# Attention probabilities of the neighbourhood layer: 32x32 block transposes on VectorE and 16 SBUF-to-SBUF DMAs per head in place of TensorE transposes and PSUM copies

## The chip, the cores and the metric

The kernel runs on one core of one Trainium2 chip. The metric is the device time of one execution, in microseconds, and the kernel before takes 1547.73 us (the median of three runs).

## The reference, cut to what matters

One step of a trunk of two layers: a layer with neighbourhood attention, then one with grouped-query attention, each followed by a gated feed-forward part. Everything is float32. The change lies in the neighbourhood attention of 512 latent tokens (a grid of 8 rows and 64 columns, 16 heads of 64): each query reads all 8 rows in a window of 16 columns, and 128 context keys, in one softmax.

```python
s_lat = jnp.einsum('brqhd,brkwhd->bhrqkw', qg, kg).astype(jnp.float32) * scale
s_lat = jnp.where(col_ok[None, None, None, :, None, :], s_lat + bias[None], -jnp.inf)
s_ctx = jnp.einsum('brqhd,bchd->bhrqc', qg, k_ctx).astype(jnp.float32) * scale
s = jnp.concatenate([s_lat.reshape(b, h, rows, GRID_W, n_lat), s_ctx], axis=-1)
p = jax.nn.softmax(s, axis=-1).astype(v.dtype)
p_lat = p[..., :n_lat].reshape(b, h, rows, GRID_W, kh, GRID_W)
p_ctx = p[..., n_lat:]
o = jnp.einsum('bhrqkw,brkwhd->brqhd', p_lat, vg) + jnp.einsum('bhrqc,bchd->brqhd', p_ctx, v_ctx)
```

Behind it come the output projection `o @ w_o`, its norm, and the feed-forward part.

## The kernel before, in words

The tokens of the grid are ordered by column, so 128 neighbouring tokens are 16 columns, and there are four such blocks, called slots. A slot's 128 queries lie on the partitions, and its keys are three blocks of 128 out of six (four of the grid, one of the prompt, one, number 5, of the context). So a head has four score tiles of 128 x 384.

`Head.scores(slot)` makes one. Two matmuls (`s<-kh,qs`, `s<-kl,qs`) write it to a PSUM bank, VectorE adds the table of bias and mask and takes the row's minimum (the scores are negated), ScalarE takes the exponential with the row's sum, VectorE takes the reciprocal, and GpSimd scales the row. The result lies in SBUF with the queries on the partitions. The values' matmul needs it the other way, with the keys on the partitions.

`Head.turns(i)` does that. Four TensorE transposes (`tp<-ident,p`) fill a PSUM bank, and one copy (`pk<-tp`, by ScalarE for i = 0 and by VectorE for 1 and 2) brings it to SBUF. A head has three such groups, 12 transposes in all. `values(two)` then multiplies for a pair of heads (`po<-pk,vt`), and ScalarE copies the outcome, in another order of the columns, into `of0[p]`, one of eight tiles that stay in SBUF, where p is the pair. Every fourth head's turn also holds the attention of the prompt's 128 tokens for four heads (steps p0, p1, p2).

TensorE's order is written by hand: the helper `pe` ties every matmul to the one before it, and the lists ORDER0, ORDER and ORDER2 say for a head h what is done in its turn. In them `s0` to `s3` are the scores of head h+1, `t0` to `t2` the transposes of head h, `v` (for an odd h) the values of the pair h-1 and h, `a` a step of the modulation's matrix product (matmuls named `ada`), and `f` a fill: a piece of the projections for later heads (`qk`, `vp`), and when these are used up, of the output projection (`y`, three matmuls of 512 columns a piece). From head 13 on ORDER2 is used. There are 26 pieces left for the heads 13 to 15.

The loads go through SP's queue: the projections' weights (`wsplit`, tiles `wr`, four buffers), the modulation's weights and later ones. A scheduler places them and the other engines' instructions by their priority and their buffers. Each engine and each queue works strictly in its order, so an instruction that waits holds up those behind it. `wsplit` rounds a weight on ScalarE (`wh`) and takes the rest on GpSimd or VectorE (`wl`). `o_split(p)` does the same with `of0[p]` (tiles `oh` and `ol`) before the output projection; it is called after head 11 for p = 0 and 1, after head 12 for 2 to 5, after head 13 for 6, and at the end for 7.

Of the kernel before, what the change touches and what calls it, by code (L numbers as in the profile page):

```python
# [39 lines left out]
NPT = 6  # L40
NPK = 6
# [8 lines left out]
ORDER0 = "f f f t0 s0 f s1 t1 f f t2 f a f f s2 s3 f f f f f".split()  # L50
# [4 lines left out]
ORDER2 = (  # L55
    "t0 s0 s1 f f f t1 f f t2 f s2 f s3 f f f f f f f".split(),
    "p0 s0 s1 f t0 f f t1 f t2 f s2 p1 f s3 v p2 f f f f".split(),
# [47 lines left out]
def hybrid_step(ctx: ExitStack, tc: tile.TileContext, A, O):  # L105
# [367 lines left out]
    of0 = [opool.tile([P, T], F32, name=f"of{p}") for p in range(KC)]  # L473
# [299 lines left out]
    with l_na:  # L773
# [161 lines left out]
        class Head:  # L935


            SRC = {
                0: ((0, 0), (1, 0)), 1: ((1, 1), (2, 0)), 2: ((2, 1), (3, 0)), 3: ((0, 1), (3, 1)),
                4: ((0, 2), (1, 2)), 5: ((2, 2), (3, 2)),  # L940
            }
            BANKS = ((4, 5), (0, 1), (2, 3))
            BLOCK = ((0, 2, 1), (0, 1, 2), (0, 2, 1), (1, 2, 0))
            TABLE = (slice(0, 7, 3), slice(1, 4), slice(1, 6, 2), slice(3, 6))

            def __init__(self, h):
                self.h, self.b = h, h % 2
                self.pts, self.t = [], {}
                self.tb = na_table(h)
                self.nm = sm.tile([P, 4], F32, name="nm")  # L950
                self.su = sm.tile([P, 4], F32, name="su")
                self.rc = sm.tile([P, 4], F32, name="rc")

            def scores(self, slot):
# [7 lines left out]
                pt = ap.tile([P, 384], F32, tag="p", name="p", bufs=NPT)  # L962
                self.pts.append(pt)
# [4 lines left out]
                nc.scalar.activation(pt, sp[:, 0:384], AF.Exp, bias=nm[:, slot : slot + 1],  # L968
                                     scale=-1.0, accum_out=su[:, slot : slot + 1])
# [3 lines left out]
                if not self.h:  # L973
                    plast[:] = [i]

            def turns(self, i):
                tp = bk.get("tp")
                for a, c in enumerate(self.BANKS[i]):
                    for j, (slot, part) in enumerate(self.SRC[c]):
                        n = self.BLOCK[slot][part]  # L980
                        turn(tp[:, (2 * a + j) * P : (2 * a + j + 1) * P],
                             self.pts[slot][:, n * P : n * P + P], ident)
                x = self.t[i] = ap.tile([P, 512], F32, tag="pk", name="pk", bufs=NPK)
                if i:
                    nc.vector.tensor_copy(x, tp)
                else:
                    nc.scalar.copy(x, tp)
                bk.put(tp)

        def values(two):  # L990
# [3 lines left out]

            def block(ov, c, x):
                for v in two:
                    rows_ = slice(64 * v.b, 64 * v.b + 64)
                    mm(ov[rows_], vt[:, c, v.h % 4, :], x(v), start=c == 5, stop=c == 3)

            block(po, 5, lambda v: v.t[0])  # L1000
            for i in (1, 2):
                for a, c in enumerate(Head.BANKS[i]):
                    ov = po[:, c * P : c * P + 256] if c < 3 else po.rearrange("p (a b) -> p a b", b=P)[:, 0::3, :]
                    block(ov, c, lambda v: v.t[i][:, a * 256 : a * 256 + 256])
            om = of0[two[0].h // 2][:, 0:NS].rearrange("p (r c) -> p r c", c=GW)
# [59 lines left out]
        for slot in range(4):  # L1065
            head.scores(slot)
            fill(slot < 3)
        for h in range(H):
# [4 lines left out]
            for i, step in enumerate(order):  # L1073
# [7 lines left out]
                elif step[0] == "t":  # L1081
                    head.turns(int(step[1]))
# [879 lines left out]
```

## Time and profile before

| what | value |
|---|---|
| time, median of 3 runs (lowest to highest) | 1547.73 us (1546.61 to 1548.59) |
| span of the profiled execution, first to last instruction | 1546.0 us |
| median of the runs less that span | 1.7 us |
| TensorE busy in the span | 1512.8 us, 98% |
| attention stage, first exponential to the last pair's values | from 69.9 to 321.4 us |
| granted TensorE clock, mean | 0.999 |

An execution's span runs from its first to its last instruction; the profile gives no other time of that execution. A group's row has the line, the engine, the operation, the tile that is written and those that are read, the shapes and the count, then its busy time and the mean of one, and the idle time of the engine before them with what ended it. A row of the timeline has the start, the duration and the count of merged instructions. Matmuls overlap, so the pace of TensorE is read from start to start. In a fp32 matmul the profile shows two passes, so the 10 matmuls of a pair's values are 20 there.

### The profile page before, as it was taken

How to read it: one execution, taken by the hardware profiler on the slowest of the kernel's cores; microseconds unless marked ns; L12 is line 12 of the kernel's file. 1: busy time of each engine (PE TensorE's matmuls, PEld its weight loads, DVE VectorE, ACT ScalarE, POOL GpSimd, SP SyncE). 2: the span in 40 equal slices, each digit the busy share in tenths (PEclk: the TensorE clock that was granted, in tenths of full speed). 3: DMA queues.
4: the chain of work that ended last, by engine and by line, in shares of the span. 5: the costliest groups of instructions: out<-in, count | busy, mean ns of one | idle time of the engine just before them, and what ended most of it. 6: DMA issues, size and time to landing. Idle time of an engine off the chain costs nothing.

```text
span 1546.0 us, 26097 instructions
## 1 busy us (share of the span) xinstructions
PE 1512.8 (98%) x9709; PEld 1344.4 (87%) x9709; DVE 1024.1 (66%) x1648; ACT 854.2 (55%) x1624; POOL 701.8 (45%) x606
## 2 busy tenths in 40 slices
PE   6999999999999999999999999999999999999998
PEld 5988998888999999978887878878899999988886
DVE  4553453659877666756757877773988887786554
ACT  5665564646655555654544447763666655554443
POOL 1554463432355455525444464532235666542433
PEclk9999999999999999999999999999999999999999
DMA  9745454253565665388574421015433334447664
GB/s 318 210 122 159 122 132 116 64 190 124 183 224 177 221 190 162 114 277 272 178 234 155 129 69 42 2 40 190 153 114 115 119 111 156 132 164 252 226 221 131
DMA packets 196666, 243.99 MB, mean 158 GB/s; under 512 B 11484, under 2 KB 153020, under 8 KB 196540
## 3 DMA queue, kind: packets, MB, share of 16 engines
q1 hardware_dynamic: 186704, 235.74, 47.7%
q10 hardware_dynamic: 9836, 6.59, 2.5%
q8 instruction: 76, 1.25, 0.3%
q14 instruction: 50, 0.41, 0.1%
HBM read 214.38 MB, written 26.34 MB: 156 GB/s over the span
## 4 chain that ended last, share of the span: by engine, by line
PE 66%; DVE 5%; ACT 2%; issue 2%; POOL 1%; DMA 1%; POOLq 0%; DVEq 0%; ACTq 0%
PE acc L117 19%; PE ux L117 18%; PE uz L117 8%; PE gp L117 5%; PE uy L117 4%; PE po L117 3%; PE y L117 3%; PE s L117 2%; PE tp L120 2%; PE ada L117 1%; DMA wr<-in_ffn_w_up 1%; DVE t L1281 1%; ACT gp L1692 1%; PE tr L120 0%; DVE xo L400 0%
## 5 line engine op out<-in xcount | busy, mean ns | idle before, releaser
L180 POOL TENSOR_TENSOR wl<-wr,wh 128x1024 fp32r<-128x1024 f32 x70 | 173.3, 2480 | 238.5 <-ACT wh L178 223.5
L1204 POOL TENSOR_TENSOR wl<-wr,wh 128x1024 fp32r<-128x1024 f32 x76 | 183.5, 2435 | 46.9 <-ACT wh L1203 43.3
L117 PE MATMUL ux<-B,wh 128*128 128x322 f32 x832 | 200.1, 311 | 0.9 <-ACT u L1258 0.9
L1281 DVE SCALAR_TENSOR_TENSOR t<-C,cw,t 128x644 f32<-128x644 f32 x176 | 156.3, 888 | 51.3 <-ACT t L1279 50.7
L117 PE MATMUL acc<-wh,alo 128*128 128x512 f32 x440 | 172.3, 392 | 0.3 <-DVE alo L1173 0.3
L178 ACT CAST wh<-wr 128x1024 fp32r<-128x1024 f32 x140 | 145.6, 1048 | 48.5 <-DMA wr<-in_ffn_w_down 37.4
L117 PE MATMUL acc<-wh,ahi 128*128 128x512 f32 x440 | 171.9, 391 | 0.0
L117 PE MATMUL acc<-wl,ahi 128*128 128x512 f32 x440 | 171.8, 391 | 0.0
L117 PE MATMUL uz<-B,wh 128*128 128x322 f32 x640 | 156.2, 312 | 0.9 <-ACT v L1258 0.9
L117 PEld LDWEIGHTS ux<-B,wh 128*128 128x128 f32 x832 | 143.6, 189 | 3.4 <-issue 1.2
L1173 DVE TENSOR_TENSOR alo<-ain,ahi 128x384 fp32r<-128x384 f32 (+1 forms) x88 | 84.0, 973 | 84.9 <-ACT ahi L1171 84.0
L117 PE MATMUL ux<-B,wl 128*128 128x322 f32 x416 | 129.5, 311 | 2.7 <-DVE wl L1204 2.7
L117 PE MATMUL qk<-hT,wh 128*128 128x384 f32 (+1 forms) x512 | 122.4, 315 | 0.0
L117 PEld LDWEIGHTS uz<-B,wh 128*128 128x128 f32 x640 | 110.9, 189 | 4.3 <-ACT v L1258 1.5
L1204 POOL TENSOR_TENSOR vl<-wr,vh 128x1024 fp32r<-128x1024 f32 x38 | 96.3, 2535 | 24.6 <-ACT vh L1203 24.3
L1203 ACT CAST wh<-wr 128x1024 fp32r<-128x1024 f32 x84 | 84.8, 1049 | 40.8 <-DVE wr L1227 40.5
L1279 ACT ACTIVATE t<-C,cw 128x644 f32<-128x644 f32 x88 | 78.6, 893 | 47.8 <-DVE C L1309 40.3
L180 DVE TENSOR_TENSOR wl<-wr,wh 128x1024 fp32r<-128x1024 f32 x70 | 91.3, 1315 | 20.1 <-ACT wh L178 19.5
L117 PE MATMUL uz<-B,wl 128*128 128x322 f32 x320 | 99.6, 311 | 0.3 <-POOL wl L1204 0.3
L117 PEld LDWEIGHTS acc<-wh,alo 128*128 128x128 f32 x440 | 82.5, 188 | 18.8 <-DVE alo L1173 1.1
L117 PEld LDWEIGHTS acc<-wl,ahi 128*128 128x128 f32 x440 | 82.6, 188 | 17.9
L117 PEld LDWEIGHTS acc<-wh,ahi 128*128 128x128 f32 x440 | 82.6, 188 | 17.8
(259 smaller groups left out, 3857.7 us busy)
## 6 DMA issues: line engine op xcount, KB each, us to landing
wr<-in_ffn_w_up SPq DMA_DIRECT2D x88, 512.0 KB
wr<-in_ffn_w_down SPq DMA_DIRECT2D x88, 512.0 KB
wr<-in_ada_w SPq DMA_DIRECT2D x72, 512.0 KB
act<-act SPq DMA_DIRECT2D x44, 321.0 KB
wr<-in_na_w_qkv SPq DMA_DIRECT2D x24, 512.0 KB
mod<-modrow SPq DMA_DIRECT2D x20, 512.0 KB
ain<-act SPq DMA_DIRECT2D x44, 192.0 KB
wf<-in_ada_w SPq DMA_DIRECT2D x16, 512.0 KB
```

The lines of the kernel that those rows point to most:

```text
L117: pe(nc.tensor.matmul(*a, **k))
L120: pe(nc.tensor.transpose(*a, **k))
L178: i = nc.scalar.copy(hi, raw)
L180: j = (low or nc.vector).tensor_sub(lo, raw, f32(hi))
L1173: pin(nc.vector.tensor_sub(lo[:, 0 : c1 - c0], ain[:, 0 : c1 - c0], f32(hi[:, 0 : c1 - c0])))
L1203: nc.scalar.copy(hl[0], src)
L1204: low.tensor_sub(hl[1], src, f32(hl[0]))
L1279: nc.scalar.activation(t, taps(0), AF.Identity, bias=cw[:, 3, n : n + 1], scale=cw[:, 1, n : n + 1])
L1281: nc.vector.scalar_tensor_tensor(t, taps(d), cw[:, w, n : n + 1], t, op0=ALU.mult, op1=ALU.add)
L1692: nc.scalar.activation(self.pt[i].rearrange("p (a b) -> p a b", a=2), sv, AF.Exp, bias=nm, scale=-1.0, accum_out=su)
```

## The change

The probabilities of a head lie in one tile `p4` of 128 x (4 x 4 x 3 x 32): for a slot, four groups k of 3 x 32 columns, so that the 32 columns of group k of each of the three key blocks stand together. The exponential writes in that order. After GpSimd's scaling VectorE transposes the tile in 32x32 blocks, in place (`nc.vector.transpose(pt, pt)`, once a slot). A block's keys then lie on the partitions of the query block q where it stood, and `exchange()` moves each of the 16 pieces of 32 partitions x 384 elements from (partitions q, group k) of `p4` to (partitions k, group q) of a second tile `px`. It is called once a head, behind the scores of slot 3, and issues its 16 DMAs on SP's queue. `values` reads `px` through an access pattern of 2 x 4 x 32 elements (`block`); the context's product, one matmul of 512 columns, becomes two of 256.

```diff
             def scores(self, slot):
...
-                nc.scalar.activation(pt, sp[:, 0:384], AF.Exp, bias=nm[:, slot : slot + 1],
-                                     scale=-1.0, accum_out=su[:, slot : slot + 1])
+                nc.scalar.activation(pt.rearrange("p k n i -> p n k i"),
+                                     sp[:, 0:384].rearrange("p (n k i) -> p n k i", n=3, k=4), AF.Exp,
+                                     bias=nm[:, slot : slot + 1], scale=-1.0, accum_out=su[:, slot : slot + 1])
...
-            def turns(self, i):
-                tp = bk.get("tp")
...
+                nc.vector.transpose(pt, pt)
+
+            def exchange(self):
+
+                self.px = ap.tile([P, 4, 4, 3, QD], F32, tag="px", name="px", bufs=NPX)
+                for q in range(4):
+                    for k in range(4):
+                        nc.sync.dma_start(self.px[QD * k : QD * k + QD, q], self.p4[QD * q : QD * q + QD, k])
+
+            def block(self, s0, s1):
+
+                c0 = 3 * QD * s0[0] + QD * s0[1]
+                c1 = 3 * QD * s1[0] + QD * s1[1]
+                return raw_ap(self.px, c0, [self.px.ap[0], [c1 - c0, 2], [12 * QD, 4], [1, QD]])
```

`p4` and `px` have two buffers each. To make room, `of0` has four buffers in place of eight tiles. The first four pairs' tiles go to DRAM after their pair, and `o_split` reads them back:

```diff
+    def of_store(p):
+
+        of0d[p] = dr.tile([P, T], F32, name=f"of0d{p}")
+        nc.sync.dma_start(of0d[p], of0.pop(p))
...
         def o_split(p):
             hi, lo = osp0[p]
-            nc.scalar.copy(hi, of0[p])
-            nc.vector.tensor_sub(lo, of0[p], f32(hi))
+            if p in of0d:
+                x = wp.tile([P, T], F32, tag="wr", name="ofr")
+                nc.sync.dma_start(x, of0d[p])
+            else:
+                x = of0[p]
+            nc.scalar.copy(hi, x)
+            nc.vector.tensor_sub(lo, x, f32(hi))
```

The lists lose the steps t0 to t2, gain `x` for the next head's exchange, and spread the scores; the number of fills in a head stays. The two of ORDER for even and odd heads:

```diff
-    "f f t0 s0 f s1 t1 f f t2 f a f f s2 s3 f f f f f f".split(),
-    "p0 f f t0 s0 f s1 t1 f t2 p1 f f f v a p2 s2 s3 f f f".split(),
+    "f s0 f f s1 f f s2 f f a f s3 f f f x f f f".split(),
+    "p0 f s0 f f s1 f p1 f f s2 f f v a p2 s3 f f x".split(),
```

Two places show what becomes of the order. The first is TensorE at the end of the stage, the last 24 projection matmuls and the values of heads 14 and 15. Before:

```order
L117 MATMUL y_3781<-wl,oh_3620 128x512
L117 MATMUL y_3781<-wh,ol_3621 128x512
L120 MATMUL tp<-ident,p 128x128 x4
L117 MATMUL y_3820<-wh,oh_3620 128x512
L117 MATMUL y_3820<-wl,oh_3620 128x512
L117 MATMUL y_3820<-wh,ol_3621 128x512
L120 MATMUL tp<-ident,p 128x128 x8
L117 MATMUL po<-pk,vt 64x512 x2
L117 MATMUL po<-pk,vt 64x256 x6
L117 MATMUL po<-pk,vt 64x2x128 x2
```

Now the same engine, from the last piece of projection to the first one behind the values:

```order
L119 MATMUL y_3804<-wh,oh_3621 128x512
L119 MATMUL y_3804<-wl,oh_3621 128x512
L119 MATMUL y_3804<-wh,ol_3622 128x512
L119 MATMUL po<-px,vt 64x256 x10
L119 MATMUL po<-px,vt 64x2x128 x2
```

The three groups of transposes of head 15 are gone, and the values stand directly behind the projection: between the scores of slot 3 of head 15 and the values are 24 matmuls `y`, where there were 27 and 12 transposes.

The second is SP's queue from the output projection's weights to the first load of the next stage (`mod`). Before:

```order
L293 DMA wr<-in_ada_w 128x1024 x2
L174 DMA wr<-in_na_w_o 128x2x512 x2
L293 DMA wr<-in_ada_w 128x1024 x2
L174 DMA wr<-in_na_w_o 128x2x512
L293 DMA wr<-in_ada_w 128x1024 x2
L174 DMA wr<-in_na_w_o 128x2x512 x4
L352 DMA mod<-modrow_2_83 128x1024
```

And now, where `px<-p` are the exchanges of the heads 12, 13, 14 and 15 and `ofr<-of0d` the tiles that come back from DRAM:

```order
L176 DMA wr<-in_na_w_o 128x2x512 x2
L994 DMA px<-p 32x384 x16
L1027 DMA ofr<-of0d_2200 128x640
L1027 DMA ofr<-of0d_2597 128x640
L994 DMA px<-p 32x384 x16
L176 DMA wr<-in_na_w_o 128x2x512 x5
L994 DMA px<-p 32x384 x32
L354 DMA mod<-modrow_2_83 128x1024
```

The exchanges now stand among the loads of one queue, those of the heads 14 and 15 behind each other and ahead of the next stage's first load. The same holds further up, where each head has its 16 between the projections' weights.

More of the change, by code (lines that the diff above doesn't have):

```diff
@@ L39 @@
 QW = T + 64
-NPT = 6
-NPK = 6
+NPT = 2
+NPX = 2
+NOF = 4
+QD = 32
 NAR = 2
@@ L1067, in hybrid_step @@
             fill(slot < 3)
+        head.exchange()
         for h in range(H):
```

63 lines of the change are left out of this document (27 added, 36 removed).

## The prediction

> **What bounds the kernel now.** I read the page first (engine shares, chain), then the table of stretches over the attention stage, then the waits of PE and of the SP queue inside that stage.
>
> ```profile
> span 1546.0 us, 26097 instructions
> PE 1512.8 (98%) x9709; PEld 1344.4 (87%) x9709; DVE 1024.1 (66%) x1648; ACT 854.2 (55%) x1624; POOL 701.8 (45%) x606
> PE 66%; DVE 5%; ACT 2%; issue 2%; POOL 1%; DMA 1%; POOLq 0%; DVEq 0%; ACTq 0%
> ```
>
> TensorE is busy for 98% of the span and carries most of the chain that ends last. The stretches of the stage (columns: length, then busy time of PE, PEld, DVE, ACT, POOL with the number of instructions, clock, DMA share, GB/s) say the same of the place that is edited:
>
> ```profile
> 100.00:150.00 50.00, 50.00 (x405) 43.97 (x403) 19.75 (x60) 27.27 (x74) 24.10 (x25) 1.00 0.52 142
> 250.00:300.00 50.00, 48.39 (x346) 41.99 (x340) 26.65 (x72) 29.91 (x78) 21.62 (x25) 1.00 0.33 91
> 300.00:330.00 30.00, 30.00 (x160) 23.87 (x159) 12.21 (x22) 14.18 (x34) 6.93 (x13) 1.00 0.18 60
> PE tp L120 <- DVE qs L878: 1.4, 2, 1.0
> SPq L174 <- POOL wl L180: 159.9, 21, 20.9
> ```
>
> PE has no idle time there to speak of (its longest wait is 1.0 us), DVE is busy for about half, and SP's queue stands still for 159.9 us, waiting for buffers of weights. So a PE instruction taken out here shortens the run by what it occupies, as long as nothing makes PE wait in its place.
>
> **What is removed.** 16 heads x 12 transposes, and three PSUM copies per head.
>
> ```profile
> L120 PE MATMUL tp<-ident,p 128*128 128x128 f32 x192 | 29.2, 273 | 2.0 <-DVE qs L878 1.4 <-POOL p L972 0.7
> 262.18 0.60 PE L120 MATMUL tp<-ident,p 128*128 128x128 f32 x4
> 262.53 0.37 PE L117 MATMUL qk<-hT,wh 128*128 128x256 f32 x1
> 262.74 0.28 PE L117 MATMUL qk<-hT,wl 128*128 128x256 f32 x1
> 262.85 0.40 PE L117 MATMUL qk<-hT,wh 128*128 128x256 f32 x2
> L985 DVE COPY pk<-tp 128x512 f32<-128x512 f32 x32 | 21.6, 685 | 9.2 <-PE tp L120 8.9
> ```
>
> The mean of 273 ns overlaps the next one, so I go by starts. Four transposes take 262.18 to 262.53 = 0.35 us, and the qk behind them takes 0.21 us to the next start, where the one after it takes 0.11: another 0.10 us lost at the change of kind. There are 48 such groups: 48 x 0.35 = 16.8 us at least, 48 x 0.45 = 21.6 at most. Three groups stand beside another group and lose less: I take **-20 us**. The DVE copies (21.6 us) and ACT's 16 stand beside PE's work and are worth nothing in themselves.
>
> **The values' matmuls.** They read px in runs of 32 elements where they read pk in one piece; the columns stay the same, 6 x 256 for 512 + 4 x 256 a head. The nearest rows of PE (qk, s) run at one pace whatever their pieces; I take 0, with -1 and +3 as ends.
>
> **What is added on DVE.** 64 block transposes of 128x384. No row shows one; the 128x512 copy above (685 ns) and the 162 ns reciprocal bound it, and 3/4 of the copy gives 0.5 us, which I take. 64 x 0.5 = 32 us of DVE against 21.6 taken away, on an engine that is half idle. But each transpose waits for POOL's scaling with DVE's next instructions (qs, kl, the next score's bias) behind it; I allow **+1.5 us** in all for PE meeting a late one, ends 0 and 8.
>
> The Trainium skill, "VectorE: DVE Perf Modes", section "Rules for kernel authors", says to transpose 128x128 on TensorE when PSUM is an acceptable destination, so it speaks against this change. Its table gives 311 ns on VectorE for a 128x128 bf16 block grid against 390 ns on TensorE; here TensorE's start-to-start is 0.35 / 4 = 88 ns. By the page's figure a 128x384 one would be an estimated 0.93 us with both ends 0.4 us later and the sum about 1 us worse; no run here shows it.
>
> **What is added on SP: the exchange.** 16 DMAs per head. The code waits for the transpose of the head's last slot, issues 16 in a row, and the values of a pair need the second head's last one to have landed. The length of that path against PE's work meanwhile decides the case. First the softmax of one slot in the trace:
>
> ```profile
> 94.95 0.34 PE L117 MATMUL s<-kl,qs 128*128 128x384 f32 x1
> 95.53 0.57 DVE L964 CUSTOM_DVE_ANT_0 s<-s,tb 128x384 f32<-128x384 f32 x1
> 96.55 0.57 ACT L968 ACTIVATE p<-s,nm 128x384 f32<-128x384 f32 x1
> 98.68 0.17 DVE L971 RECIPROCAL rc<-su 128x1 f32<-128x1 f32 x1
> 99.10 0.59 POOL L972 TENSOR_SCALAR p<-p,rc 128x384 f32<-128x384 f32 x1
> ```
>
> From the score's end (95.3) to POOL's end (99.7) are 4.4 us; without the queues in between the durations alone make 2.2. With the transpose I take 4.7 us, ends 3 and 6.5. Then the issue of 16 DMAs, by the nearest rows of SP's queue (duration min/median/max in ns, first and last start), and how long after an issue the last one lands:
>
> ```profile
> L1169 SPq DMA_DIRECT2D ain<-act x88: 319/347/1398, 639.0 to 1521.2; - x88
> L1564 SPq DMA_DIRECT2D gkh<-gkh x12: 590/590/1025, 846.5 to 866.0; - x12
> 82.66 0.82 SPq L293 DMA_DIRECT2D wr<-in_ada_w  x2
> 863.94 0.59 SPq L1564 DMA_DIRECT2D gkl<-gkl  x1
> 864.62 0.59 SPq L1564 DMA_DIRECT2D gkh<-gkh  x1
> SPq L1958 <- DMA out_y_prompt<-xo: 1.6, 1, 1.6
> ```
>
> px is 32 partitions of one run of 384 elements. ain is the nearest in shape (rows of up to 384 elements, 0.35 us; two plain loads in a row take 0.82, so **0.40 us** from one to the next). gkh is the nearest in kind (SBUF to SBUF), but has three dimensions on both sides: 0.68 us from one to the next. I take 0.40 and keep 0.68. Landing: 1.6 us for 256 KB. The path is 4.7 + 15 x 0.40 + 0.35 + 1.6 = **12.7 us**.
>
> Now PE's work meanwhile. Period of a pair of heads, and what it holds:
>
> ```profile
> 99.81 2.81 PE L117 MATMUL po<-pk,vt 128*64 128x512 f32 x20 [0.24 <-DVE qs L878]
> 102.54 1.07 PE L117 MATMUL ada<-wr,scolp 128*32 128x256 f32 x16
> 104.41 0.34 PE L117 MATMUL s<-kl,qs 128*128 128x384 f32 x1
> 104.59 0.34 PE L117 MATMUL s<-kh,qs 128*128 128x384 f32 x1
> 266.33 2.81 PE L117 MATMUL po<-pk,vt 128*64 128x512 f32 x20
> ```
>
> Five periods are 266.33 - 99.81, one is 33.3 us. Less six groups of transposes (2.7), the values (2.8), eight slots at 2 x 0.18 (2.9) and two ada steps (2.1) leaves 22.8 us for 24 fills: 0.95 each. In the changed orders 14 fills and 3 slots stand between an odd head's slot 3 and the values: 14 x 0.95 + 1.1 = **14.4 us**. That hides 12.7, by 1.7 us, for the six pairs up to head 11: **0**.
>
> The pair 12/13 has less: 36 y matmuls, 8 prompt scores, 3 slots and a prompt transpose. The tail has the least: 24 y, since the fills run out.
>
> ```profile
> 313.13 0.39 PE L117 MATMUL y<-wh,oh 128*128 128x512 f32 x1
> 316.31 0.39 PE L117 MATMUL y<-wh,ol 128*128 128x512 f32 x1
> 317.68 1.03 PE L120 MATMUL tp<-ident,p 128*128 128x128 f32 x8
> 318.64 2.81 PE L117 MATMUL po<-pk,vt 128*64 128x512 f32 x20
> ```
>
> From 313.13 to 316.31 are 14 steps of y: 0.23 us each. Pair 12/13: 36 x 0.23 + 8 x 0.11 + 1.1 + 0.4 = 10.7, so PE waits 12.7 - 10.7 = **+2.0 us**. Pair 14/15: 24 x 0.23 = 5.5, so it waits 12.7 - 5.5 = **+7.2 us**; before, eight transposes stood there and nothing waited. All of SP's later loads (mod, the up-projection's first weights) stand behind these exchanges, but a wait of PE moves the time they are needed as well: 0.
>
> A long pause may also cost speed. At the run's start PE comes out of one:
>
> ```profile
> 17.77 3.64 PE L120 MATMUL tr<-ident,x 128*128 128x128 f32 x16 [1.54 <-DVE x L541]
> 21.34 2.24 PE L117 MATMUL row<-wf,scolp 128*32 128x256 f32 x32
> 33.52 1.93 PE L117 MATMUL row<-wf,scolp 128*32 128x256 f32 x32
> ```
>
> Sixteen transposes take 3.64 us, 0.23 each against 0.12 in the 317.68 row; after those 3.6 us the pace is nearly the later one (2.24 against 1.93). So some 1.8 us go after a long pause: **+1.5 us** for the tail's, ends 0 and 3. The granted clock in the stretches is 1.00 all along and shows none of it. The Trainium skill, "TensorE: Matmul & The Clock Gate", section "Why this matters for your kernels", says that idle gaps above some 3 us drop the array to half its clock; the slow transposes agree with it, and without that rule the sum would be 1.5 us lower.
>
> The four of-tiles that go to DRAM and come back are 8 DMAs on SP. The reloads for heads 4 to 7 stand behind px of head 12 on SP, ahead of their splits on ACT and DVE: I reckon them at 0, because the fills that need them come after the prompt scores, with an end of +3.
>
> **Sum.** -20 + 1.5 + 2.0 + 7.2 + 1.5 = **-7.8 us**. Against the profiled execution's span of 1546.0: 1538.2. The shown runs' median is 1547.73, 1.7 us above that span, so the forecast is **1540 us**.
>
> **Rivals.**
> 1. *SP's issue becomes the bound* (slower). If each exchange DMA costs what gkh costs, the path is 4.7 + 15 x 0.68 + 0.59 + 1.6 = 17.1 us. Six pairs wait 17.1 - 14.4 = 2.7 (16), pair 12/13 waits 6.4, and the tail 11.6 plus about 3 because px of head 14 is still being issued; with eight pauses of 1 us of slow clock that is +45 - 20 = +25: 1573 us. For it: the only SBUF-to-SBUF rows. Against: kinds with a plain 2-D shape all cost 0.32 to 0.35. From the forecast, the wins are used up at an issue of about 0.55 us: the two ends take 30 us per us of issue, and the six pairs 90 more from 0.51 us on.
> 2. *Half-way: the gain is given back.* The softmax path is 6.5 us, since DVE waits for a POOL that is in a weight split, and the issue costs 0.43. The path is then 15.0 us: six pairs wait 0.6 each (3.5), both ends 2.3 more (4.5): -7.8 + 8 is no change, 1548, with 1545 to 1552 around it. For it: the row of 99.10, where POOL came late. Against: the 1.7 us in hand.
> 3. *All is hidden.* The path is 10 us (softmax 3, landing 0.8, issue 0.39): the tail waits 4.5, nothing else does, the clock stays: 1546.0 - 21 + 4.5 + 1.7 = 1531.
> That the change doesn't do what it says is excluded by the order of PE, which has no tp of p left.
>
> **How the numbers follow.** Forecast (1536 to 1544) 0.48, rival 1 0.25, rival 2 0.20, rival 3 0.07. About 0.2%, 3 us, is what a measurement here can tell from no change. Faster takes the forecast less 0.04 at its edge, rival 3 and 0.02 of rival 2: 0.53. Same takes 0.04 and 0.11: 0.15. Slower takes the rest of rival 2 and rival 1: 0.32. The two sides both weigh, so: the forecast's own range is 1536 to 1544, and the one that leaves 2 in 10 out is **1532 to 1565** (it takes in the lower part of rival 1).
>
> **What would show it.** Right: no tp of p, PE idle before po only, nearly all of it in the last pair (7 us) and the one before (2 us), px issues 0.40 us apart, the six earlier pairs without a wait. Wrong: px issues 0.6 us apart and PE waiting for a DMA at every po (rival 1); DVE idle for POOL's scaling and PE waiting for qs or kl (rival 2); a transpose near 0.9 us.

## The result, and the profile after

The changed kernel takes 1592.6 us (median of five runs, 1590.9 to 1596.6), against 1547.9 us for the kernel before beside it: 1.0292 times the time, 95% interval 1.0280 to 1.0305. The forecast was 1540 us with a range from 1532 to 1565. It is 45 us slower, and beyond the rival that had the sign right (1573 us).

The page of the changed kernel, its span, its engines and its chain:

```profile
span 1590.1 us, 26190 instructions
PE 1510.3 (95%) x9549; PEld 1338.5 (84%) x9549; DVE 1036.0 (65%) x1680; ACT 845.3 (53%) x1608; POOL 700.0 (44%) x606
PE 62%; DVE 6%; ACT 2%; issue 2%; POOL 1%; DMA 1%; POOLq 0%; DVEq 0%; ACTq 0%; SPq 0%
```

TensorE's busy time fell by 2.5 us only although 192 transposes are gone: matmuls at a lower clock count as busy for longer. (In a run below without exchange and turns, where the clock of the stage is 1.00, it is 1492.3 us, 20.5 less than before.) The waits of TensorE from 60 to 372 us (sum, times, longest) and two stretches (columns as in the prediction) say what it lost:

```profile
PE po L119 <- DMA px<-p: 32.4, 8, 9.6
PE s L119 <- DVE qs L892: 5.6, 1, 5.6
PE tp L122 <- POOL pp L708: 4.0, 2, 2.2
...
100.00:150.00 50.00, 39.77 (x309) 35.24 (x309) 18.53 (x53) 21.15 (x56) 22.70 (x23) 0.94 0.61 161
...
350.00:376.00 26.00, 16.40 (x76) 12.26 (x76) 5.92 (x5) 8.63 (x18) 6.69 (x7) 0.80 0.52 160
```

Before, no wait here was above 1.0 us and the clock was 1.00. Now there are 32.4 us of waits for `px`, some 16 us of other ones, and a granted clock of 0.94 and, at the end, 0.80. The values of four pairs on the timeline; the last score and the last turn of the second pair's odd head; and SP's queue around that pair and at the end:

```profile
107.93 2.78 PE L119 MATMUL po<-px,vt 128*64 128x256 f32 x22 [0.96 <-DMA px<-p]
147.57 4.57 PE L119 MATMUL po<-px,vt 128*64 128x256 f32 x22 [8.14 <-DMA px<-p]
329.43 3.10 PE L119 MATMUL po<-px,vt 128*64 128x256 f32 x23
360.10 4.13 PE L119 MATMUL po<-px,vt 128*64 128x256 f32 x22 [9.60 <-DMA px<-p]
...
125.08 0.34 PE L119 MATMUL s<-kl,qs 128*128 128x384 f32 x1
129.45 0.58 DVE L987 STREAM_TRANSPOSE p<-p 128x384 f32<-128x384 f32 x1 [0.72 <-POOL p L984]
...
115.82 14.69 SPq L994 DMA_DIRECT2D px<-p  x16
130.61 1.37 SPq L295 DMA_DIRECT2D wr<-in_ada_w  x2
132.08 13.67 SPq L994 DMA_DIRECT2D px<-p  x16
...
338.25 20.21 SPq L994 DMA_DIRECT2D px<-p  x32
```

At the second pair, the even head's exchange holds SP from 115.82 to 130.51, the odd head's starts only behind it and ends at 145.75, and TensorE goes on at 147.57, 1.8 us later. At five of the eight pairs the same 22 matmuls take 4.1 to 4.6 us behind their wait in place of 2.78: the pause costs a second time, through the clock. Around the second pair the granted clock is 0.50 in each stretch of 1 us from 147 to 151 us, 0.89 in the next and then 1.00. The whole of `px` on SP's queue (ns min/median/max) and two of SP's waits from 60 to 376 us:

```profile
L994 SPq DMA_DIRECT2D px<-p x256: 507/588/1545, 78.9 to 357.9; - x128
SPq L994 <- DMA wr<-in_ada_w: 10.7, 8, 3.4
SPq L176 <- POOL wl L182: 10.4, 3, 8.2
```

An issue takes 0.59 us, and 16 in a row 10.0 us at best, 0.63 apart; where they also wait for earlier loads it is up to 14.7. SP had 159.9 us to spare in front of buffers of weights and now has 10.4. That row (SP's line of the weights waiting for `wl`) is used below as the measure of SP's slack.

The other new wait, in the order of time:

```profile
78.17 2.52 POOL L941 TENSOR_TENSOR tb<-mask,tr 128x256 f32<-128x256 f32 x3
80.65 2.36 POOL L182 TENSOR_TENSOR wl<-wr,wh 128x1024 fp32r<-128x1024 f32 x1
82.99 0.58 POOL L984 TENSOR_SCALAR p<-p,rc 128x384 f32<-128x384 f32 x1
83.61 0.58 DVE L987 STREAM_TRANSPOSE p<-p 128x384 f32<-128x384 f32 x1 [3.49 <-POOL p L984]
87.39 0.66 PE L119 MATMUL s<-kh,qs 128*128 128x384 f32 x1 [5.63 <-DVE qs L892]
```

GpSimd is in the tables of the next heads and a weight split, so the scaling comes late, the turn behind it makes VectorE wait 3.49 us, and `qs`, which stands behind the turn, makes TensorE wait 5.63 us. A turn itself takes 0.58 us.

### The profile page after: what moved, and what is told of

Its sections match the earlier page's. It is cut to its first block, busy times and chain, and to the rows that moved or that the text cites. A ratio compares the mean times of both kernels' runs of the same rounds, so it can differ in the third digit from the quotient of the medians.

```text
span 1590.1 us, 26190 instructions
## 1 busy us (share of the span) xinstructions
PE 1510.3 (95%) x9549; PEld 1338.5 (84%) x9549; DVE 1036.0 (65%) x1680; ACT 845.3 (53%) x1608; POOL 700.0 (44%) x606
## 4 chain that ended last, share of the span: by engine, by line
PE 62%; DVE 6%; ACT 2%; issue 2%; POOL 1%; DMA 1%; POOLq 0%; DVEq 0%; ACTq 0%; SPq 0%
PE acc L119 18%; PE ux L119 16%; PE uz L119 8%; PE gp L119 5%; PE uy L119 4%; PE po L119 2%; PE y L119 2%; PE s L119 2%; PE tp L122 2%; PE ada L119 1%; DMA wr<-in_ffn_w_up 1%; DVE t L1298 1%; ACT gp L1709 1%; DVE al L1221 0%; ACT t L1296 0%
## 5 line engine op out<-in xcount | busy, mean ns | idle before, releaser
L119 PEld LDWEIGHTS acc<-wh,ahi 128*128 128x128 f32 x440 | 82.6, 188 | 17.7
```

What stands on the lines that cost most here:

```text
L119: pe(nc.tensor.matmul(*a, **k))
```

## The experiments

All are edits of the changed kernel; the line numbers in their rows are their own. Ratios are to the kernel before, run beside them. Those that leave out the exchange or the turns, or move its pieces straight across or by halves, do not compute the full result.

### Without the exchange

```diff
-NPT = 2
+NPT = 4
...
-                self.px = ap.tile([P, 4, 4, 3, QD], F32, tag="px", name="px", bufs=NPX)
-                for q in range(4):
-                    for k in range(4):
-                        nc.sync.dma_start(self.px[QD * k : QD * k + QD, q], self.p4[QD * q : QD * q + QD, k])
+                self.px = self.p4
```

> Leaves out the exchange: the values' matmuls read each head's turned blocks where they are (no DMA, four buffers of p in place of two of p and two of px). The turns on VectorE and all waits for GpSimd's scaling stay. Theory A (the 16 DMAs per head on SP's queue, 0.59 us each, hold PE at the values): all of the 32 us of PE waits for px go, and with them the half-speed stretches behind them; left is the gain of the transposes taken out, less what the turns cost: 1526 to 1535 us. Theory B (VectorE's turns waiting in order for GpSimd hold up the score chain, and with it everything): 1570 us or more, since that part stays. Theory C (the values' matmuls themselves are slower, by reading px in runs of 32): po rows stay at 4 us in place of 2.8, 1555 us or more.

1548.4 us, 0.9998 (0.9988 to 1.0007). The exchange costs 1592.6 - 1548.4 = 44 us. But without it the kernel is not faster than before, against the 1526 to 1535 us of theory A; its waits of TensorE:

```profile
PE tp L122 <- POOL pp L708: 5.0, 4, 2.6
PE s L119 <- DVE qs L892: 4.9, 1, 4.9
...
L119 PE MATMUL po<-p,vt 128*64 128x256 f32 x192 | 22.5, 383 | 1.9 <-DVE qs L892 1.9
```

So the gain of 20 us is lost to something else, and theory C is out: a `po` matmul takes 383 ns, as long as the 256-column ones before (379).

### The same bytes, 4 DMAs a head

```diff
                 for q in range(4):
-                    for k in range(4):
-                        nc.sync.dma_start(self.px[QD * k : QD * k + QD, q], self.p4[QD * q : QD * q + QD, k])
+                    nc.sync.dma_start(self.px[:, q], self.p4[:, q])
```

> The same bytes (768 KB a head) go from p to px, but by 4 DMAs of 128 partitions x 384 elements in place of 16 of 32 x 384; the pieces are copied straight across, not exchanged. Theory A, in the form that a DMA from SBUF to SBUF costs SP some 0.6 us whatever its size: an exchange takes 2.5 us of SP in place of 10 to 14, only the tail pair waits (3 to 5 us): 1530 to 1540 us. Theory D (the bytes: moving 768 KB from SBUF to SBUF beside the weights' loads is what takes the time): stays at 1585 to 1595 us.

1549.7 us, 1.0009 (1.0000 to 1.0018): within 1.3 us of no exchange at all, and with the changed kernel's two buffers of p, so the four buffers of the run above were not what helped. The bytes cost nothing that can be told; the 43 us above it come with the step from 4 to 16 DMAs.

```profile
L993 SPq DMA_DIRECT2D px<-p x64: 464/593/1678, 78.3 to 315.1; - x64
```

A DMA of four times the size takes SP the same 0.59 us. (The forecast of 1530 to 1540 had the lost 20 us in it too.)

### 16 DMAs of another shape

```diff
-                        nc.sync.dma_start(self.px[QD * k : QD * k + QD, q], self.p4[QD * q : QD * q + QD, k])
+                        nc.sync.dma_start(self.px[:, q, k], self.p4[:, q, k])
```

> Again the same bytes, by 16 DMAs a head as in the change, but each of 128 partitions x 96 elements, straight across. Theory A by count (a price per DMA): px issues stay 0.6 us apart and the time stays within 5 us of the changed kernel, 1588 to 1600 us. If instead the price comes from the narrow shape (32 partitions, so few rows for the engines to share), an issue falls to 0.35 to 0.4 us and the time to about 1540 to 1560 us.

1575.8 us, 1.0175 (1.0158 to 1.0192), between the two forecasts.

```profile
L994 SPq DMA_DIRECT2D px<-p x256: 464/599/1523, 75.2 to 343.3; - x128
```

The price of an issue is the same, so the narrow shape is not the cause. The 17 us less go with an earlier start: a DMA here reads one slot alone, and the first ones of a head leave before its last slot is done (SP's waits for the turn are 15.2 us in place of 37.3). This run changes two things against the changed kernel, so that these 17 us are due to the start is not shown. Against the run with four DMAs, which copies straight across too, the 16 DMAs cost 26 us in spite of the earlier start.

### 8 DMAs a head

```diff
-                    for k in range(4):
-                        nc.sync.dma_start(self.px[QD * k : QD * k + QD, q], self.p4[QD * q : QD * q + QD, k])
+                    for k in range(2):
+                        nc.sync.dma_start(self.px[64 * k : 64 * k + 64, q], self.p4[64 * (1 - k) : 128 - 64 * k, q])
```

> The same bytes by 8 DMAs a head of 64 partitions x 384 elements (the two halves swapped, not the exchange of 32-blocks). Theory A2 (SP's time, some 0.65 us per DMA): an exchange takes 5 to 6 us of SP, two of them 11 of 33 us, which leaves room: close to the run with four DMAs, with 3 to 6 us at the last pair: 1550 to 1558 us. If the loss grows in step with the number of DMAs (1550 us at 4, 1593 at 16): about 1564 us.

1558.7 us, 1.0068 (1.0055 to 1.0081), just above the 1550 to 1558 us of A2 and below the 1564 of a price in step with the count. The same bytes thus take 1549.7, 1558.7 and 1592.6 us in 4, 8 and 16 DMAs: four more than 4 cost 9 us, and eight more than 8 another 34. SP's slack (its wait for `wl`) is 62.1, 32.3 and 10.4 us in the three.

### Without the turns

```diff
-                nc.vector.transpose(pt, pt)
```

> Leaves out the 64 block transposes on VectorE; the 16 DMAs a head stay and wait for GpSimd's scaling instead. Theory A: the exchange starts 0.6 to 1 us earlier at each of the eight pairs, and the one score that waited 5.6 us for qs behind a turn comes in time: 8 to 15 us less than the changed kernel, 1577 to 1585 us; the 16 issues stay as long. Theory B: most of the loss goes, 1560 us or less.

1582.1 us, 1.0227 (1.0204 to 1.0249), 10 us below the changed kernel, inside theory A. TensorE's waits for `px` stay at 30.6 us.

### Neither exchange nor turns

```diff
-                nc.vector.transpose(pt, pt)
...
+                self.px = self.p4
```

> Leaves out both the exchange and the turns on VectorE: the values read the scaled p where it is, and nothing of the change is left but the 192 transposes taken off TensorE. If the prediction's term of -20 us is right, and the run without the exchange (1548 us) gave it all back through VectorE's turns that wait in order for GpSimd: 1524 to 1532 us, with no PE wait over 2 us in the stage. If the transposes on TensorE were worth less than reckoned (5 us or so, since PE cannot run through the rest faster than its inputs come): 1540 us or more.

1538.7 us, 0.9937 (0.9919 to 0.9955), between the two. The turns cost 1548.4 - 1538.7 = 10 us, and the transposes gave 9 us, not 20. What is left of waits in the stage:

```profile
PE tp L122 <- POOL pp L708: 5.7, 2, 3.1
PE tk L122 <- ACT kp L906: 1.7, 1, 1.7
PE qk L119 <- DVE qs L892: 1.2, 1, 1.2
```

These are 8.6 us, where the kernel before has 3.0 us of waits. The clock is below 1.00 in four of the stretches from 60 to 376 us (0.95, 0.98, 0.97 and 0.93), an estimated 6 us at most. Together that is 11 to 12 us for the 11 that are missing. `pp` is the softmax of the prompt's four heads. Before, three groups of transposes stood between its scores (p0) and its turn (p1), besides the same four fills and two slots.

### The prompt's turn later

```diff
-    "p0 f s0 f f s1 f p1 f f s2 f f v a p2 s3 f f x".split(),
+    "p0 f s0 f f s1 f f f p1 s2 f f v a p2 s3 f f x".split(),
```

(the same in ORDER2, on the kernel with neither exchange nor turns)

> Leaves out exchange and turns, as the run at 1539 us did, and moves the prompt's four transposes two fills later in the order of the odd heads. There PE waited 5.7 us for GpSimd's pp, which 12 transposes a head had covered in the kernel before. If that lost cover is why only 9 of the 20 us came through: that wait falls below 1.5 us and the time to 1531 to 1535 us. If PE loses the time elsewhere as soon as it runs faster: 1537 us or more.

1536.1 us, 0.9923 (0.9906 to 0.9939); the wait for `pp` falls to 1.9 us and the clock of the stage is 1.00 throughout. A part of the lost cover, 2.6 us, comes back. The run misses its forecast by 1 us: 7.9 us of waits are left, spread over the stage, 1.9 of them for `pp`.

### The scaling on VectorE

```diff
-                i = nc.gpsimd.tensor_scalar(pt, pt, rc[:, slot : slot + 1], 1.0, op0=ALU.mult, op1=ALU.mult)
-                if not self.h:
-                    plast[:] = [i]
+                nc.vector.tensor_scalar(pt, pt, rc[:, slot : slot + 1], 1.0, op0=ALU.mult, op1=ALU.mult)
```

(without the exchange; what `plast` orders is tied to a table of head 1 instead)

> Without the exchange, as in the first run, but the scaling of p by 1/sum moves from GpSimd to VectorE, directly ahead of the turn, so that no VectorE instruction waits for GpSimd's queue; VectorE gets 64 instructions of some 0.56 us more. Theory B1 (the 20 us went into the in-order wait for GpSimd): the PE waits for qs, kl and pp fall from 16 to below 5 us: 1528 to 1536 us. Theory B2 (it is VectorE's added load itself): with 36 us more on VectorE it gets no better than 1548, rather 1550 us or more.

1543.9 us, 0.9972 (0.9960 to 0.9983): 4.5 us of the 10 come back although VectorE has more to do, which neither forecast has. A `s` still waits 3.3 us for `qs`; the row of all the scalings and a place on the timeline show why:

```profile
L986 DVE TENSOR_SCALAR p<-p,rc x64: 380/421/2510, 72.6 to 310.4; 128x384 f32<-128x384 f32 x64
...
78.47 2.40 POOL L182 TENSOR_TENSOR wl<-wr,wh 128x1024 fp32r<-128x1024 f32 x1 [1.07 <-ACT wh L180]
78.57 2.51 DVE L986 TENSOR_SCALAR p<-p,rc 128x384 f32<-128x384 f32 x1
```

A scaling of 0.42 us takes 2.51 us when it starts 0.1 us behind GpSimd's weight split, and ends 0.2 us after it. It is no single case: the 18 scalings that start while a weight split runs all end 0.21 to 0.23 us behind it. With the scaling moved, VectorE no longer waits for GpSimd's result, but here still for GpSimd.

### Each turn one slot later

```diff
+                while late:
+                    late.pop(0)()
                 nc.vector.reciprocal(rc[:, slot : slot + 1], su[:, slot : slot + 1])
...
-                nc.vector.transpose(pt, pt)
+                late.append(lambda: nc.vector.transpose(pt, pt))
```

(without the exchange; the last one is issued where the exchange stood)

> Without the exchange, as in the first run; GpSimd keeps the scaling, but the turn of a slot is issued on VectorE only after the next slot's bias and maximum (where VectorE waits for ScalarE's exp in any case), not right behind its own scaling. The same work on every engine. Theory B1 (the 10 us between the runs with and without turns, 1548 and 1539 us, are VectorE waiting in order for GpSimd): back to 1539 to 1543 us. If it is the 37 us of turns themselves: 1546 us or more.

1549.3 us, 1.0006 (0.9996 to 1.0015). It says nothing on either theory, since the edit did not do what it was for: VectorE's idle time ahead of the turns for the scaling is 56.1 us, against 55.7 without the edit. At the place shown above the turn is still ahead of `qs` and waits 3.52 us. The scheduler orders VectorE's instructions, and it left this turn where it was.

### One turn a head, where the exchange stood

```diff
-                nc.vector.transpose(pt, pt)
...
+                nc.vector.transpose(self.p4, self.p4)
+                self.px = self.p4
```

> Without the exchange, as in the first run (1548 us), in the order of the changed kernel; the four turns of each head become one VectorE instruction of 128x1536 where the exchange stood, two or three fills behind the last score. Theory B1 (a VectorE queue that stands behind a late GpSimd scaling is what the turns cost): most of the 10 us between 1548 and 1539 come back, 1539 to 1544 us. If the turns cost by their length: VectorE has 16 x 1.78 = 28 us in place of 37, so at most 2 us come back, 1546 us or more.

1548.7 us, 1.0008 (0.9999 to 1.0017): nothing comes back. That is outside theory B1 and inside the forecast by length (1546 us or more).

```profile
L990 DVE STREAM_TRANSPOSE p<-p 128x1536 f32<-128x1536 f32 x16 | 28.5, 1779 | 17.7 <-POOL p L984 17.7
...
89.45 1.67 POOL L941 TENSOR_TENSOR tb<-mask,tr 128x256 f32<-128x256 f32 x2 [4.47 <-DMA tr<-in_k_rpb]
91.09 0.59 POOL L984 TENSOR_SCALAR p<-p,rc 128x384 f32<-128x384 f32 x1
91.71 1.78 DVE L990 STREAM_TRANSPOSE p<-p 128x1536 f32<-128x1536 f32 x1 [4.21 <-POOL p L984]
93.98 0.33 PE L119 MATMUL sp<-kl,qs 128*128 128x128 f32 x1 [4.04 <-DVE kl L864]
```

VectorE's waits for the scaling fell from 55.7 to 17.7 us in sum, and the time did not follow. What counts are the few long ones: here GpSimd waits 4.47 us for a table's load, the scaling and the turn stand behind it, and `kl` behind the turn, so that one TensorE wait of 4.9 us was only exchanged for one of 4.0. This shows why the late turn did not help; it does not exclude that the length of the turns counts as well.

### Through DRAM, 5 DMAs

```diff
+                d = dr.tile([P, 16 * 3 * QD], F32, name=f"pd{self.h}")
+                nc.sync.dma_start(d, self.p4.rearrange("p a b c d -> p (a b c d)"))
+                w = 12 * QD
+                for k in range(4):
+                    nc.sync.dma_start(
+                        self.px[QD * k : QD * k + QD].rearrange("p q s n j -> p q (s n j)"),
+                        raw_ap(d, w * k, [[4 * w, QD], [4 * w * QD, 4], [1, w]]),
+                    )
```

> The exchange made through DRAM: one write of 768 KB and four reads of 192 KB a head, 5 DMAs on SP in place of 16. Five issues of 0.4 to 0.6 us are 2 to 3 us, and the two landings (read after write) an estimated 2 x 2 to 4 us, worked out from 256 KB loads that land in 1.6 us: a path of 6 to 11 us behind the last turn. Theory A (the number of DMAs on SP): the six inner pairs do not wait, the last pair 3 to 6 us: 1548 to 1558 us, since the 20 us given back by the turns remain. Rival (a DMA behind a DMA costs as much as ten issues): px waits stay above 20 us, 1575 us or more.

1609.4 us, 1.0407 (1.0384 to 1.0429). Theory A's forecast is wrong here, and the rival holds: TensorE waits 39.2 us for `px`. The issues are cheap:

```profile
L996 SPq DMA_DIRECT2D px<-pd x64: 302/424/1455, 82.8 to 373.9; - x64
L993 SPq DMA_DIRECT2D pd<-p x16: 326/327/345, 78.2 to 369.3; - x16
...
122.94 0.33 SPq L993 DMA_DIRECT2D pd<-p  x1
129.88 1.74 SPq L996 DMA_DIRECT2D px<-pd  x4
```

But the reads must wait for the write, and SP waits with them, 6.9 us here, with the loads behind it standing still. A few long DMAs on the path cost as much as many short ones.

### Every second DMA from ScalarE's queue

```diff
-                        nc.sync.dma_start(self.px[QD * k : QD * k + QD, q], self.p4[QD * q : QD * q + QD, k])
+                        (nc.scalar if k % 2 else nc.sync).dma_start(
+                            self.px[QD * k : QD * k + QD, q], self.p4[QD * q : QD * q + QD, k])
```

> The 16 DMAs of a head as in the change, every second one issued from ScalarE's queue. Theory A (the issue on one queue, one after the other): the issue falls from 10 us to about 5 a head and px waits to below 10 us; but ScalarE, in order, then waits for the turn and spends 8 x 0.6 = 4.8 us a head on issuing, with qs, kh and exp behind it: 1560 to 1580 us. Rival (a limit that both queues share): px waits stay at 30 us, 1590 us or more.

1616.3 us, 1.0442 (1.0420 to 1.0464). The waits for `px` fall from 32.4 to 6.4 us, as theory A said, but its time of 1560 to 1580 us was wrong: the kernel is slower than with one queue.

```profile
PE tk L122 <- ACT kp L906: 20.8, 4, 7.9
...
ACT kp L906 <- DMA px<-p: 35.0, 3, 13.5
ACT vt L501 <- DMA px<-p: 30.2, 3, 10.7
```

ScalarE's copies stand behind its share of the exchange for up to 13.5 us at a time.

### The values later

```diff
-    "f s0 f f s1 f f s2 f f a f s3 f f f x f f f".split(),
-    "p0 f s0 f f s1 f p1 f f s2 f f v a p2 s3 f f x".split(),
+    "f s0 f f s1 f v X f s2 f f a f s3 f f f x f f f".split(),
+    "p0 f s0 f f s1 f p1 f f s2 f f a p2 s3 f f".split(),
```

(X is the exchange of the even head itself, behind the values of the pair ahead of it; the tail's orders have all fills that are left ahead of the last values)

> The changed kernel with all 16 DMAs a head, in another order: the values of a pair come some 6 fills later (in the next even head), the even head's exchange is issued behind them, and the last pair's values stand behind all output fills that are left. Nothing is taken out. Theory A (the length of the path from the last score to the values against PE's work meanwhile): with some 6 us more cover at the inner pairs and 15 us more at the last, PE's waits for px fall from 34 to below 8 us, and the time to 1548 to 1560 us, the level of the run without an exchange plus a little. If SP is simply too full (two exchanges of 10 to 14 us and the loads in a period of 33 us), px or weights come late elsewhere: 1570 us or more.

1589.3 us, 1.0263 (1.0248 to 1.0278). The waits for `px` fall to 9.1 us, and the time by 3 us only: theory A, as the length of one head's path, is wrong, and the time is that of the other forecast, an SP that is too full (1570 us or more).

```profile
PE po L119 <- DMA px<-p: 9.1, 4, 7.2
PE vp L119 <- POOL wl L182: 8.8, 1, 8.8
...
262.10 0.85 POOL L941 TENSOR_TENSOR tb<-mask,tr 128x256 f32<-128x256 f32 x1 [9.64 <-DMA tr<-in_k_rpb]
```

What waits instead is a projection, and many small ones. The projection's weight split `wl` stands on GpSimd behind a table. That table's load was issued from ScalarE's queue from 251.94 us on and the table starts at 262.10, while five loads of weights, which SP had issued from 251.17 us on behind two exchanges, came in too (the DMA share is 0.81 to 1.08 from 254 to 262 us). That the exchanges made these loads late is read from the order of SP's queue; no run separates it.

### The values later, with the scaling on VectorE and the prompt's turn later

```diff
-                i = nc.gpsimd.tensor_scalar(pt, pt, rc[:, slot : slot + 1], 1.0, op0=ALU.mult, op1=ALU.mult)
+                nc.vector.tensor_scalar(pt, pt, rc[:, slot : slot + 1], 1.0, op0=ALU.mult, op1=ALU.mult)
```

(and `f f f p1` in place of `f p1 f f`, on top of the orders above)

> As the run with the delayed values, and further the scaling of p on VectorE ahead of the turn, and the prompt's transposes two fills later. If the three losses add up (exchange hidden, 4 us for the scaling, 4 us for the prompt): 1538 to 1548 us, at or a little below the kernel before. If SP stays the bound: within 5 us of the run with the delay alone.

1580.3 us, 1.0204 (1.0188 to 1.0219). The two further edits give 9 us together, where they gave 4.5 and 2.6 alone, and the time is outside both forecasts. Of the 32 us that are left above the kernel before, the longest waits are `px` with 8.8 us and `vp` with 7.7 for `wl`; the rest is not broken down.

### Half of the heads exchanged

The even heads are turned on VectorE and exchanged, the odd ones use `turns` of the kernel before, in its order.

```diff
-    "f s0 f f s1 f f s2 f f a f s3 f f f x f f f".split(),
-    "p0 f s0 f f s1 f p1 f f s2 f f v a p2 s3 f f x".split(),
+    "f f s0 f s1 f f f a f f s2 s3 f f f f f f".split(),
+    "p0 f f t0 s0 f s1 t1 f t2 p1 f f f v a p2 s2 s3 f f f x".split(),
```

> Half of the change: even heads are turned on VectorE and exchanged by 16 DMAs, odd heads stay on TensorE with transposes and copies as in the kernel before, in the order of the kernel before. SP then has one exchange of 10 to 14 us in a period of 33 us in place of two, and an even head's px has a whole head's time until the values. Theory A2 (SP's queue is too full with two exchanges a period; the path of one head would not matter if SP had time): PE's waits for px below 3 us in all, SP is again held by buffers of weights for over 60 us in the stage, as it was for 160 in the kernel before; the time is -10 us for 24 groups of transposes, +5 for half of the turns, +0 to 3: 1540 to 1546 us. If the latency of an exchange alone decides (even one a period): px waits above 10 us, 1555 us or more.

1559.1 us, 1.0072 (1.0054 to 1.0090). On SP theory A2 holds: no wait of TensorE for `px` is left, and SP waits for weights' buffers again (59.6 us). The time misses by 13 us, for another reason:

```profile
PE po L119 <- issue: 12.6, 3, 5.7
...
98.18 0.86 POOL L941 TENSOR_TENSOR tb<-mask,tr 128x256 f32<-128x256 f32 x1 [3.92 <-DMA tr<-in_k_rpb]
99.01 0.59 POOL L992 TENSOR_SCALAR p<-p,rc 128x384 f32<-128x384 f32 x1
99.63 0.58 DVE L996 STREAM_TRANSPOSE p<-p 128x384 f32<-128x384 f32 x1 [4.33 <-POOL p L992]
103.92 0.23 DVE L892 SCALAR_TENSOR_TENSOR qs<-qk,qs 64x64 fp32r<-64x64 f32 x1
...
104.24 0.66 PE L119 MATMUL po<-px,vt 128*64 128x256 f32 x1 [5.65 <-issue]
```

The wait is put down to "issue", but VectorE's row shows where it comes from. A table's load is late, GpSimd's table and scaling behind it, VectorE's turn waits 4.33 us for that, and two copies `pk`, the next turn and the last `qs` stand behind it. TensorE goes on 0.09 us after that `qs` ends (104.15 us), and 0.10 us after the same `qs` at the two other waits of this row (171.68 and 241.50 us); that it waits for the `qs` is inferred from this.

### Half of the heads, one late turn

```diff
-                nc.vector.transpose(pt, pt)
...
             def exchange(self):
+                nc.vector.transpose(self.p4, self.p4)
...
-    "f f s0 f s1 f f f a f f s2 s3 f f f f f f".split(),
+    "f X f s0 f s1 f f f a f f s2 s3 f f f f f f".split(),
```

> As the run with half of the heads exchanged, but the four slots of an even head are turned by one VectorE instruction of 128x1536 (2.3 us by four times 0.58) one fill into the next head's time, when GpSimd's scaling should have ended. Theory B1 (VectorE's in-order wait for GpSimd is what the turns cost): 2 to 4 us less than the run with four turns a head, 1537 to 1543 us. If the turns cost by their own length on VectorE, the same as that run or, since 2.3 us in one piece block qs and the bias, up to 3 us more.

1544.3 us, 0.9974 (0.9963 to 0.9985): the full computation, faster than both kernels, and 15 us faster than with four turns a head, where theory B1 had forecast 2 to 4; its range of 1537 to 1543 us is missed by 1 us. The exchange starts later together with the turn, so the run moves both.

```profile
PE po L119 <- issue: 1.4, 1, 1.4
...
SPq L176 <- POOL wl L182: 58.2, 12, 8.1
```

Four turns in one take 1.78 us in place of 2.31, and the wait of 12.6 us is 1.4.

### The same, one fill later still

```diff
-    "f X f s0 f s1 f f f a f f s2 s3 f f f f f f".split(),
-    "p0 f f t0 s0 f s1 t1 f t2 p1 f f f v a p2 s2 s3 f f f".split(),
+    "f f X s0 f s1 f f f a f f s2 s3 f f f f f f".split(),
+    "p0 f f t0 s0 f s1 t1 f t2 f p1 f f v a p2 s2 s3 f f f".split(),
```

> As the run with half of the heads exchanged and one late turn (1544 us), with that turn one fill later still and the prompt's transposes one fill later. PE's waits left in the stage there are 8 us, of which the late kp, kl and po (5 us) stand behind VectorE or ScalarE: if the turn still waits for GpSimd somewhere, 1 to 3 us less, 1541 to 1544 us; if not, the same within 2 us.

1545.6 us, 0.9979 (0.9969 to 0.9988): the same within the intervals.

## Why the prediction was wrong, point by point

- **The sum.** It had -20 (transposes) + 1.5 (turns) + 9.2 (exchange at both ends) + 1.5 (clock). Measured one after the other: transposes -9, turns +10, exchange with its clock +44, which is the +45 of the result. The rows of the changed kernel agree: 48.7 us of waits from 60 to 372 us where there were 3.0, the -20 of the transposes, and a clock below 1.00 in all seven stretches of the stage, which is worth an estimated 21 us at most (from these means).
- **The exchange's path: the step that failed.** It took 0.40 us from one issue to the next, after `ain`, "the nearest in shape", and kept the 0.68 of `gkh`, "the nearest in kind", for a rival. The kind was right: 0.59 us an issue and at least 0.63 apart. For `px` it does not depend on the shape: 32 x 384, 128 x 96, 64 x 384 and 128 x 384 all have medians of 0.59 or 0.60. At the second pair the path is 22.2 us for the forecast's 12.7: from the score's end (125.42 us) to the turn's end 4.6 (forecast 4.7), then 2.1 behind the even head's exchange and two loads (0), 13.7 for the issues (6.35) and 1.8 to TensorE (1.6). TensorE's work meanwhile is 14.0 us (14.4), so the wait is 8.1. The softmax, the cover and the landing (1.4 to 1.8 us behind the last issue at the seven pairs that wait) were right; the issue and the place in the queue were not.
- **The path was taken for one head's alone.** This made the loss larger than rival 1's. The 16 exchanges hold SP for 186 us (the sum of their rows) between 79 and 358 us, two in a period (33.3 us before), and the odd head's waits for the even head's and for loads. Of the 32.4 us, the six inner pairs, forecast at 0, waited 20 (rival 1: 16), and the last pair 12 (forecast 7.2, rival 14.6); 12/13 waited not at all (forecast 2.0). That two exchanges a period are too much for SP is shown by the half exchange (slack 59.6 us, no `px` wait left) and by the run with the values later, where more cover took 23 us of `px` waits away and only 3 us of time. That the weights behind the exchanges are what costs there is argued, not shown. In the changed kernel itself no matmul from 60 to 372 us waits for a weight, and the first one behind waits 2.0 us where it waited 1.4, so the 0 for SP's later loads was near.
- **The transposes, -20.** The working of their length is not refuted. In the run with the prompt's turn later, at a clock of 1.00, 12.3 us gained and 4.9 us more of waits than before make 17 us, inside the working's 16.8 to 21.6, and TensorE's busy time is 20.5 us less. What failed is "as long as nothing makes PE wait in its place". The transposes had covered the prompt's softmax and others; that the 8.6 us of waits in the run with neither are lost cover is shown for the prompt's turn alone (5.7 to 1.9 us when it was moved).
- **The turns, +1.5 with an end of 8.** The mechanism was named, a transpose waiting for GpSimd with `qs` and `kl` behind it, and the size was off: 10 us. The length was near (0.58 us for 0.5). The forecast's estimate of 0.93 us, from the 311 ns that the Trainium skill's "VectorE: DVE Perf Modes", section "The three transpose paths", gives for 128x128 bf16, is refuted by the trace for 128x384 fp32.
- **The clock, +1.5 at the tail.** It is paid at five of the eight pairs: 4.1 to 4.6 us for 2.78, each after a wait of 2.4 us or more. The forecast had read that the granted clock shows none of it; in this profile it does (0.80 from 350 to 376 us, with waits of 9.6 and 2.3). That agrees in the main with the rule of the Trainium skill quoted there, though here waits of 2.4 and 2.9 us, below its some 3 us, were enough, while in the run without the turns a wait of 3.12 us was followed by matmuls at the full pace (2.77 us): no run here gives a fixed threshold. The forecast's own rows did not show a pause either: the slow transposes at 17.77 us come behind a wait of 1.54 us, and those from 9.65 us on are as slow.
- **The values' 32-element runs, 0**, was right. **The tiles through DRAM, 0**, was not tried by itself; the version at 1544.3 us has them too.

What stays open: why the 10 us of the turns do not come back in the changed order. With half of the heads, one late turn gained 15 us, and its rows show the wait that went. In the full order one late turn only moved the long wait to another place, and the run that was to move each turn did not move it. A price of the turns by their length is thus not excluded there, although scaling on VectorE, which gives it more work, got 4.5 us back.

## What to carry to other kernels

Where the row nearest in kind and the one nearest in shape have different prices (0.59 and 0.35 us here), do not take the cheaper one, and then add up the whole queue per period, not the path of one use: a queue that has time to spare hides an exchange, and in a full one each exchange also waits for the one ahead of it. Before taking instructions off the bounding engine, list which softmax, copy or load they covered, since a part of the gain is paid back there. An instruction that waits for another engine in order belongs where that engine is surely done; with half of the heads, one late instruction for four early ones made the difference between slower and faster; in the full order it gained nothing.

## What was not expected of the hardware

- An issue of a DMA from SBUF to SBUF takes SP 0.59 us for 48 KB as for 192 KB, one from SBUF to DRAM 0.33, and one from DRAM to SBUF of 192 KB 0.42. The tables' loads (`tr`, DRAM to SBUF, with three dimensions) take 0.61, so such a price is not a mark of SBUF to SBUF alone.
- VectorE's scaling of 128x384 (fp32, SBUF to SBUF) takes 0.42 us alone and up to 2.51 us when it starts while GpSimd is in a weight split (tensor-tensor), ending 0.21 to 0.23 us after it, while the block transpose in the same run never took over 0.581. The Trainium skill, "SBUF — State Buffer", section "Who interferes with whom", has the two share a pair of ports as an exclusive lock that such a VectorE form can take; the rows agree.
- A block transpose of 128x1536 takes 1.78 us, four of 128x384 take 2.31: an estimated 0.18 us of each is fixed.
